# One PEER layer, 128 blocks of H: sixteen spilled blocks change operand form, and eight more blocks are spilled

## The chip, the cores and the metric

The kernel runs on one core of one Trainium2 chip. The metric is the device time of one execution in microseconds (us); the median of the runs counts, and lower is better.

## The reference, cut to what matters

Two transformer blocks on 512 tokens with d = 1024. The first ends in a PEER layer, a mixture of 16384 single-neuron experts, and the change lies there:

```python
def peer_sublayer(h, g_ffn, w_peer_q, keys_1, keys_2, peer_u, peer_v):
    x = rmsnorm(h, g_ffn)
    q = (x @ w_peer_q).reshape(T, 8, 128)                  # 8 heads
    s1, s2 = q[..., :64] @ keys_1.T, q[..., 64:] @ keys_2.T  # 128 scores each
    v1, i1 = lax.top_k(s1, 16); v2, i2 = lax.top_k(s2, 16)
    cand = v1[..., :, None] + v2[..., None, :]             # 256 candidates
    sc, ci = lax.top_k(cand, 16)
    eidx = i1[ci // 16] * 128 + i2[ci % 16]                # 128 experts per token
    gates = softmax(sc)
    act = gelu(einsum('td,tkd->tk', x, peer_u[eidx]))
    return einsum('tk,tkd->td', gates * act, peer_v[eidx])
```

## The kernel before, in words

The last 384 tokens (`ND`; the first 128 are `T0`) go through the layer densely. For each of 128 blocks `j` of 128 experts a block of H, `gelu(U_j x)`, 128 x 384, is formed, multiplied by a dense matrix of gates, and multiplied by `V_j` into the output. The first 128 tokens gather their rows of U and V one by one with indirect DMAs (`gather`, `gstep`), paced along the rest.

`hblock` forms one block of H: `wload` loads 512 KB of U and splits it into a high half (a cast, L166, on ScalarE = ACT) and a low half (a subtraction, L167, on GpSimd = POOL or on VectorE = DVE), `mm3` (L185 to L187) multiplies three pairs of halves, high x high, low x high and high x low, in 8 steps over d: 24 matmuls of 128x384 with operands of the split type, float32r. ACT applies gelu (L716). A block that is formed ahead of its turn is *spilled*: `hspill` writes it to DRAM (`h_d`), and the main loop reads it back. `SP` spreads the numbers of the spilled blocks evenly over the 128. For spilled blocks the subtraction is on POOL.

The stages around the change follow one another in `phase2`:

- **norm_apply** (L215 ff.) multiplies the residual by gain and norm for each half of the tokens: `hf`, a temporary in the ring of the H blocks (tag `hg`, 8 buffers), from which the halves `xnh` (L222, ACT) and `xnl` (L223, DVE) of the whole x are made.
- **Query stage**: 8 heads. A 512-column product with `w_pq` gives q; for each of 4 token tiles the scores (L808, native float32, 256 columns) are copied by ACT (L810) and DVE selects the 16 largest of each 128 (`top16`, L783 to L788). After heads 2 and 5 (`QH`) one block is spilled. After head 3, `xg` is built by ACT and POOL for the first 128 tokens and transposed to `xt`.
- **Index decoding**: for each of 4 token tiles DVE adds candidates (L848), selects 16 of 80 for each head, and turns their places into expert numbers by a chain of small operations (L865 to L895). At four places of each tile (`TK_H`) a block is spilled: 16 blocks. `spread` transposes indices and gates of a tile for the next stage.
- **One-hot stage**: for each of 48 groups of 8 tokens DVE builds one-hot matrices A (L920) and B (L940), 128x2048 in fp16, and TensorE multiplies them (L928) into the dense gates, which go to DRAM (`g_d`). After every second group a block is spilled: 24 blocks. A has 4 buffers, B has 3.
- 6 more blocks (`TR_H`), and then the **main loop** over the 128 j: `stage_a` forms a block or reads a spilled one, `stage_b` multiplies by gates and splits V, `stage_c` (L990) runs 18 matmuls of 512 columns.

2 + 16 + 24 + 6 = 48 blocks (`NS`) are spilled. A scheduler sets the order of each engine's instructions from this program and the pools: U's raw buffers ("row") are 3, its halves 3 (`UB`), the accumulators of H ("mm") 2.

Of the kernel before, what the change touches and what calls it, by code (L numbers as in the profile page):

```python
# [9 lines left out]
F32 = mybir.dt.float32  # L10
# [5 lines left out]
AF = mybir.ActivationFunctionType  # L16
OP = mybir.AluOpType
# [143 lines left out]
def psum(S, tag, bufs, shape=(128, 512), name=None):  # L161
    return S.ps.tile([128, 512], F32, name=name or tag, tag=tag, bufs=bufs)
# [7 lines left out]
def wload(S, pool, src, kc, m, tag="w", raw=2, bufs=2, rtag=None, eng=None):  # L170
    nc = S.nc
    r = pool.tile([128, kc * m], F32, name=tag + "r", tag=rtag or tag + "r", bufs=raw)
    nc.sync.dma_start(r, src.rearrange("p k m -> p (k m)"))
    hi = pool.tile([128, kc * m], F32R, name=tag + "h", tag=tag + "h", bufs=bufs)
    lo = pool.tile([128, kc * m], F32R, name=tag + "l", tag=tag + "l", bufs=bufs)
    split(S, hi, lo, r, eng)
    f = lambda t: t.rearrange("p (k m) -> p k m", m=m)
    return f(hi), f(lo)


def mm3(S, out, w, x, kc, xs, ws=slice(None)):

    mm = S.nc.tensor.matmul
    for k in range(kc):
        mm(out, w[0][:, k, ws], x[0][:, k, xs], start=k == 0, stop=False)  # L185
        mm(out, w[0][:, k, ws], x[1][:, k, xs], start=False, stop=False)  # L186
        mm(out, w[1][:, k, ws], x[0][:, k, xs], start=False, stop=k == kc - 1)  # L187
# [27 lines left out]
def norm_apply(S, R, hs, nr, a, sh, hi, lo, get):  # L215

    nc = S.nc
    col = lambda k: 0.0 if sh is None else sh[:, k:k + 1]
    for k in range(8):
        t = get()  # L220
        nc.vector.scalar_tensor_tensor(t, R[:, k, hs], a[:, k:k + 1], nr, op0=OP.mult, op1=OP.mult)
        nc.scalar.activation(hi[:, k, hs], t, AF.Identity, bias=col(k))  # L222
        nc.vector.scalar_tensor_tensor(lo[:, k, hs], t, col(k), hi[:, k, hs].bitcast(F32), op0=OP.add, op1=OP.subtract)  # L223
# [426 lines left out]
ND = 384  # L650
T0 = 128
GT, GJ, GPB = 32, 4, 3
HGB, NR, NG, VRB = 8, 3, 5, 5
LA, LB = 5, 4
LT = 3
QH = (2, 5)
PQE = 1
UB = 3
LATE = 7
TK_H = (2, 6, 8, 9)  # L660
TK_G = ()
TR_H = 6
G_H = 1
G_G = 0
NS = len(QH) + 4 * len(TK_H) + ND // 16 * G_H + TR_H
SP = [i * NJ // NS for i in range(NS)]


# [24 lines left out]
def phase2(S, ctx, R, gains, early=lambda S: None):  # L693

    nc, tc, ap = S.nc, S.tc, S.ap
    mm, V = nc.tensor.matmul, nc.vector
    pools = ExitStack()
    pool = lambda n, st=pools: st.enter_context(tc.tile_pool(name=n, bufs=1, reuse_waits="tile"))
    pu, xn = S.pu, S.xn
# [5 lines left out]
    nc.gpsimd.memset(yt, 0.0)  # L705
    g_d = S.dr.tile([ND // GT, 128, NJ, GT], F32, name="g_d")
    h_d = S.dr.tile([NJ, 128, ND], F32, name="h_d")
    for x, hs in enumerate(HALF):
        norm_apply(S, R, hs, S.nr[x], gains, None, xn[0], xn[1], lambda: pu.tile([128, ND], F32, name="hf", tag="hg", bufs=HGB)[:, :256])

    def hblock(j, eng=None):
        w = wload(S, pu, ap["u"][j], 8, 128, tag="u", raw=NR, bufs=UB, rtag="row", eng=eng)
        p = psum(S, "mm", 2)[:, :ND]
        mm3(S, p, w, xn, 8, slice(T0, 512))
        hg = pu.tile([128, ND], F32, name="hg", tag="hg", bufs=HGB)
        S.last_gelu = nc.scalar.activation(hg, p, AF.Gelu)  # L716
        return hg

    nh = [0]

    def hspill(n=1):
        for _ in range(n):
            nc.sync.dma_start(h_d[SP[nh[0]]], hblock(SP[nh[0]], nc.gpsimd))
            nh[0] += 1

    def gather(k, src, s):
# [34 lines left out]
    def gstep(n=1):  # L761
        for _ in range(n):
            x = next(gs, None)
            if x:
                x[0](x[1])
                gdone[0] += 1

    with tc.tile_pool(name="tk", bufs=1, reuse_waits="tile") as pt_:
# [9 lines left out]
        with tc.tile_pool(name="tq", bufs=1, reuse_waits="tile") as pq:  # L778
            T = lambda tag, n, b=2, dt=F32: pq.tile([128, n], dt, name=tag, tag=tag, bufs=b)
# [12 lines left out]
            for h in range(8):  # L792
                if h == 0:
                    ps = [psum(S, "mm", 2) for _ in range(2)]
                    for hs in HALF:
                        for w, p in zip(S.first, ps):
                            mm3(S, p[:, hs], w, xn, 8, hs)
                if h < 2:
                    p = ps[h]
                else:  # L800
                    w = wload(S, pu, ap["w_pq"][h], 8, 128, tag="u", raw=NR, bufs=UB, rtag="row", eng=PQE and nc.gpsimd)
                    p = psum(S, "mm", 2)
                    mm3(S, p, w, xn, 8, slice(None))
                qT = T("qT", 512)
                nc.scalar.copy(qT, p)
                for t in range(4):
                    p = psum(S, "st", 2)
                    mm(p[:, :256], qT[:, 128 * t:128 * t + 128], kb, start=True, stop=True)  # L808
                    s = pq.tile([128, 256], F32, name="s", tag="s", bufs=4)
                    nc.scalar.copy(s, p[:, :256])  # L810
                    for e in range(2):
                        top16(s[:, 128 * e:128 * e + 128], 128, VV[t][:, e, h], II[t][:, e, h])
                if h in QH:
                    hspill()
                if h == 3:
                    for k in range(8):
                        t = T("xg", 128, 3)
                        nc.scalar.mul(t, R[:, k, :T0], gains[:, k:k + 1])
                        nc.gpsimd.tensor_tensor(t, t, S.nr[0][:, :T0], op=OP.mult)
                        if k % 4 == 0:  # L820
                            p = psum(S, "pt", 1)
                        nc.tensor.transpose(p[:, 128 * (k % 4):128 * (k % 4) + 128], t, S.ident)
                        if k % 4 == 3:
                            nc.scalar.copy(xt[:, 128 * (k - 3):128 * (k + 1)], p)

# [17 lines left out]
            for t in range(4):  # L843
# [8 lines left out]
                for h in range(8):  # L852
                    hs = slice(16 * h, 16 * h + 16)
                    top16(cand[:, h], 80, sc[:, hs], ci[:, hs])
                    if h in TK_H:
                        hspill()
                    if late and h == LATE:
                        spread(top[0])
                    if t and h in TK_G:
                        anchor[0] = None  # L860
                        gstep()
# [20 lines left out]
                for e in range(2):  # L882
                    eq = pq.tile([128, 128, 16], BF, name="eq", tag="eq", bufs=1)
                    V.tensor_tensor(eq, abb[:, e, :, None].to_broadcast([128, 128, 16]), iob[:, None, :16].to_broadcast([128, 128, 16]), op=OP.is_equal)
                    if 8 + e in TK_H:
                        hspill()
                    if t and 8 + e in TK_G:
                        gstep()
                    e4 = eq.rearrange("p (h k) a -> p h k a", k=16)
                    V.tensor_tensor(e4, e4, IB[:, e, :, None, :].to_broadcast([128, 8, 16, 16]), op=OP.mult)  # L890
                    for n in (8, 4, 2):
                        V.tensor_tensor(eq[:, :, :n], eq[:, :, :n], eq[:, :, n:2 * n], op=OP.add)
                    V.tensor_tensor(e12[e][:, :, None], eq[:, :, 0:1], eq[:, :, 1:2], op=OP.add)
# [14 lines left out]
                else:  # L908
                    late.append((t, e12, gt))
                    if t == 3:  # L910
                        spread()

        tg = ExitStack()
        pt_ = pool("tg", tg)
        tok = lambda x, t: x[:, t // 8].rearrange("p e (r q) -> p (e r) q", q=2)[:, :, None, :].to_broadcast([128, 8, 128, 2])
# [18 lines left out]
        for n in range(ND // 8 + 1):  # L934
            if n < ND // 8:
                t, b = T0 + 8 * n, n % (GT // 8)
# [15 lines left out]
    hspill(TR_H)  # L952
    assert nh[0] == NS

    ngl = 256 - gdone[0]
    with tc.tile_pool(name="pv", bufs=1, reuse_waits="tile") as pv:
# [47 lines left out]
        get = lambda: pv.tile([128, 1024], F32, name="ys", tag="vr", bufs=VRB)  # L1004
        ys = [yt, None, None, None]
        for x, hs in enumerate(HALF):
# [6 lines left out]
            for k in range(0, 8, 2):  # L1013
                p = psum(S, "mm", 2)
# [93 lines left out]
def open3(S):  # L1108

    nc, g3 = S.nc, S.g3  # L1110
    S.p3 = ExitStack()
    pool = lambda n: S.p3.enter_context(S.tc.tile_pool(name=n, bufs=1, reuse_waits="tile", side="right"))
    S.pn = pn = pool("p3n")
    S.pw = pool("p3w")
    S.ng3 = pn.tile([128, N_GAINS3], F32, name="ng3")
    nc.vector.tensor_scalar(S.ng3, g3, -1.0, None, op0=OP.mult)
    S.modb = pn.tile([128, 48], F32, name="modb")
    nc.vector.tensor_tensor(S.modb, S.mod, g3[:, :48], op=OP.add)
    S.ga = []
    for e, g in ((1, G_N1), (4, G_N2)):  # L1120
        a = pn.tile([128, 8], F32, name=f"ga{e}")
        nc.vector.tensor_scalar(a, S.modb[:, 8 * e:8 * e + 8], 1.0, -1.0, op0=OP.add, op1=OP.mult)
        nc.vector.tensor_tensor(a, a, g3[:, g:g + 8], op=OP.mult)
        S.ga.append(a)
    S.hf = lambda: pn.tile([128, 256], F32, name="hf", tag="hf", bufs=3)
    S.hf()
    S.first = [wload(S, S.pw, S.ap["w_in2"][4 + e], 8, 128, raw=RAW) for e in range(2)]

# [320 lines left out]
```

## Time and profile before

| | |
|---|---|
| median of 3 runs | 2544.19 us (2543.97 to 2545.87) |
| profiled execution | 2549.88 us, span 2548.1 us, mean granted TensorE clock 0.984 |
| TensorE (PE) busy | 2443.6 us, 96% of the span |
| VectorE (DVE) busy | 1807.9 us, 71% |
| ScalarE (ACT) busy | 1050.5 us, 41% |
| GpSimd (POOL) busy | 651.9 us, 26% |
| DMA | 439.59 MB read, 45.09 MB written, 190 GB/s over the span |

In the span of the profiled execution the query stage lies at about 592 to 667 us, index decoding at 667 to 797, the one-hot stage at 797 to 955, and the main loop's matmuls of L990 at 998 to 1846. Busy shares over the whole span average stages in which different engines work without a pause.

### The profile page before, as it was taken

How to read it: one execution, taken by the hardware profiler on the slowest of the kernel's cores; microseconds unless marked ns; L12 is line 12 of the kernel's file. 1: busy time of each engine (PE TensorE's matmuls, PEld its weight loads, DVE VectorE, ACT ScalarE, POOL GpSimd, SP SyncE). 2: the span in 40 equal slices, each digit the busy share in tenths (PEclk: the TensorE clock that was granted, in tenths of full speed). 3: DMA queues.
4: the chain of work that ended last, by engine and by line, in shares of the span. 5: the costliest groups of instructions: out<-in, count | busy, mean ns of one | idle time of the engine just before them, and what ended most of it. 6: DMA issues, size and time to landing. Idle time of an engine off the chain costs nothing.

```text
span 2548.1 us, 35084 instructions
## 1 busy us (share of the span) xinstructions
PE 2443.6 (96%) x13173; PEld 2078.4 (82%) x13173; DVE 1807.9 (71%) x3335; ACT 1050.5 (41%) x1727; POOL 651.9 (26%) x440
## 2 busy tenths in 40 slices
PE   7999999999966799999999999999999999999999
PEld 6778888788856689888888888888877777888887
DVE  6666777659999784888887877878655655755532
ACT  5664333544333454333333333333353663544421
POOL 2101111123344563444443443444100001000000
PEclk9999999999988899999999999999999999999999
DMA  5213664651335569999999999998321212222332
GB/s 202 76 41 131 200 205 159 211 186 64 111 103 162 234 235 349 353 361 341 327 329 327 335 328 333 317 334 311 115 76 34 79 54 75 71 95 91 97 103 89
DMA packets 188538, 486.99 MB, mean 191 GB/s; under 512 B 16359, under 2 KB 81272, under 8 KB 186704
## 3 DMA queue, kind: packets, MB, share of 16 engines
q1 hardware_dynamic: 148736, 341.74, 39.8%
q0 software_dynamic: 39632, 143.00, 15.6%
q8 instruction: 103, 1.69, 0.3%
q14 instruction: 67, 0.55, 0.1%
HBM read 439.59 MB, written 45.09 MB: 190 GB/s over the span
## 4 chain that ended last, share of the span: by engine, by line
PE 82%; DVE 12%; ACT 2%; DMA 1%; POOL 1%; issue 1%; SPq 0%; DVEq 0%; ACTq 0%; POOLq 0%
PE mm L185 13%; PE mm L186 13%; PE mm L187 13%; PE sq L990 7%; PE st L990 7%; PE o L990 3%; PE pt L990 3%; PE st L186 2%; PE st L185 2%; PE st L187 2%; PE mm L1417 2%; PE mm L1416 2%; PE mm L1418 2%; PE st L928 1%; PE o L454 1%
## 5 line engine op out<-in xcount | busy, mean ns | idle before, releaser
L185 PE MATMUL mm<-xnh,uh 128*128 128x384 f32 (+2 forms) x1104 | 379.8, 344 | 17.9 <-ACT hg L716 17.9
L187 PE MATMUL mm<-xnh,ul 128*128 128x384 f32 (+2 forms) x1104 | 380.0, 344 | 11.8 <-POOL ul L167 11.8
L186 PE MATMUL mm<-xnl,uh 128*128 128x384 f32 (+2 forms) x1104 | 379.4, 344 | 0.1
L166 ACT CAST uh<-ur 128x1024 fp32r<-128x1024 f32 x136 | 143.0, 1053 | 318.5 <-PE mm L186 228.4
L167 DVE TENSOR_TENSOR wl<-wr,wh 128x1024 fp32r<-128x1024 f32 (+2 forms) x132 | 147.9, 1121 | 177.5 <-ACT wh L166 176.7
L728 POOL DMA_INDIRECT gr<-in_u_rows,iu x128 | 184.7, 1443 | 233.3 <-DVE yt L745 180.4
L728 POOL DMA_INDIRECT gr<-in_v,iv x128 | 176.9, 1382 | 233.6 <-DVE gr L741 193.7
L185 PEld LDWEIGHTS mm<-xnh,uh 128*128 128x128 f32 x1104 | 212.1, 192 | 23.6 <-ACT hg L716 18.6
L187 PEld LDWEIGHTS mm<-xnh,ul 128*128 128x128 f32 x1104 | 212.0, 192 | 14.4 <-POOL ul L167 12.4
L186 PEld LDWEIGHTS mm<-xnl,uh 128*128 128x128 f32 x1104 | 212.3, 192 | 5.9 <-DVE xnl L223 0.4
L166 ACT CAST wh<-wr 128x1024 fp32r<-128x1024 f32 (+2 forms) x132 | 126.7, 961 | 210.3 <-PE mm L1417 87.7
L167 POOL TENSOR_TENSOR ul<-ur,uh 128x1024 fp32r<-128x1024 f32 x54 | 171.2, 3180 | 140.6 <-ACT uh L166 139.5
L166 ACT CAST wh<-gj 128x384 fp32r<-128x384 f32 x128 | 65.7, 513 | 292.6 <-issue 150.2
L745 DVE SCALAR_TENSOR_TENSOR yt<-gr,act,yt 128x1024 f32<-128x1024 f32 x128 | 163.9, 1281 | 0.2
L167 DVE TENSOR_TENSOR vl<-vr,vh 128x1024 fp32r<-128x1024 f32 x128 | 156.0, 1219 | 4.4 <-ACT vh L166 4.0
L186 PE MATMUL mm<-xnl,wh 128*128 128x512 f32 (+2 forms) x400 | 156.4, 392 | 0.5 <-DVE xnl L223 0.4
L185 PE MATMUL mm<-xnh,wh 128*128 128x512 f32 (+2 forms) x400 | 156.6, 392 | 0.2 <-ACT wh L166 0.2
L741 DVE SCALAR_TENSOR_TENSOR gr<-gr,xt 128x1024 f32<-128x1024 f32 x128 | 155.7, 1219 | 0.4 <-DMA gr<-in_u_rows,iu 0.4
L187 PE MATMUL mm<-xnh,wl 128*128 128x512 f32 (+2 forms) x400 | 154.8, 388 | 0.5 <-DVE wl L167 0.5
L167 DVE TENSOR_TENSOR wl<-gj,wh 128x384 fp32r<-128x384 f32 x128 | 71.1, 556 | 115.5 <-ACT wh L166 102.3
L167 DVE TENSOR_TENSOR ul<-ur,uh 128x1024 fp32r<-128x1024 f32 x82 | 100.5, 1226 | 56.7 <-ACT uh L166 46.1
L166 ACT CAST vh<-vr 128x1024 fp32r<-128x1024 f32 x128 | 134.8, 1053 | 4.7 <-issue 3.3
(729 smaller groups left out, 6080.3 us busy)
## 6 DMA issues: line engine op xcount, KB each, us to landing
ur<-in_u SPq DMA_DIRECT2D x128, 512.0 KB
vr<-in_v SPq DMA_DIRECT2D x128, 512.0 KB
adaw<-in_w_ada SPq DMA_DIRECT2D x48, 512.0 KB
g_d<-gb SPq DMA_DIRECT2D x12, 2048.0 KB
gp<-g_d SPq DMA_DIRECT2D x32, 768.0 KB
wr<-in_w_in SPq DMA_DIRECT2D x45, 512.0 KB
wr<-in_w_up SPq DMA_DIRECT2D x44, 512.0 KB
wgr<-in_w_in SPq DMA_DIRECT2D x24, 512.0 KB
```

What stands on the lines that cost most here:

```text
L166: S.nc.scalar.copy(hi, src)
L167: (eng or S.nc.vector).tensor_tensor(lo, src, hi.bitcast(F32), op=OP.subtract)
L185: mm(out, w[0][:, k, ws], x[0][:, k, xs], start=k == 0, stop=False)
L186: mm(out, w[0][:, k, ws], x[1][:, k, xs], start=False, stop=False)
L187: mm(out, w[1][:, k, ws], x[0][:, k, xs], start=False, stop=k == kc - 1)
L728: op = nc.gpsimd.indirect_dma_start(out=r, out_offset=None, in_=src, in_offset=bass.IndirectOffsetOnAxis(ap=idx[k][:, s:s + 1], axis=0))
L741: paced(V.scalar_tensor_tensor(r, r, 1.0, xt, op0=OP.mult, op1=OP.mult, accum_out=act[:, s:s + 1]))
L745: paced(V.scalar_tensor_tensor(yt, r, act[:, s:s + 1], yt, op0=OP.mult, op1=OP.add))
L990: mm(Y[2 * t + e], W[w_][:, c], vv[v_][:, 512 * e:512 * e + 512], start=n == 0 and w_ + v_ == 0, stop=n == NJ - 1 and w_ == 1)
L1416: mm(p, w[0][:, k], gb[2 * f], start=f == 0, stop=False)
L1417: mm(p, w[0][:, k], gb[2 * f + 1], start=False, stop=False)
L1418: mm(p, w[1][:, k], gb[2 * f], start=False, stop=f == 21)
```

## The change

The blocks spilled in the query stage go from one after heads 2 and 5 to 0, 1, 1, 2, 1, 2, 1, 2 after the eight heads: 10 instead of 2, so 56 in all, and the main loop forms 72 blocks and reads 56. The 16 blocks of the decoding stage go through a new `hblock_whole`: it neither casts nor subtracts, and multiplies the raw U with the whole normalised x in 8 matmuls of native float32. That x must now be kept: `norm_apply` writes it to a tile `xr`, 128x8x512 float32, in a pool of its own that is closed before the one-hot stage's pool opens. The transposes after head 3 read `xr`, so `xg` and its sixteen operations are gone.

```diff
     for k in range(8):
-        t = get()
+        t = get(k)
         nc.vector.scalar_tensor_tensor(t, R[:, k, hs], a[:, k:k + 1], nr, op0=OP.mult, op1=OP.mult)
...
-QH = (2, 5)
+QH = (0, 1, 1, 2, 1, 2, 1, 2)
...
-NS = len(QH) + 4 * len(TK_H) + ND // 16 * G_H + TR_H
+NS = sum(QH) + 4 * len(TK_H) + ND // 16 * G_H + TR_H
...
+    xrs = ExitStack()
+    xr = xrs.enter_context(tc.tile_pool(name="xr", bufs=1, reuse_waits="tile", side="right")).tile([128, 8, 512], F32, name="xr")
     for x, hs in enumerate(HALF):
-        norm_apply(S, R, hs, S.nr[x], gains, None, xn[0], xn[1], lambda: pu.tile([128, ND], F32, name="hf", tag="hg", bufs=HGB)[:, :256])
+        norm_apply(S, R, hs, S.nr[x], gains, None, xn[0], xn[1], lambda k: xr[:, k, hs])
...
+    def hblock_whole(j):
+
+        w = pu.tile([128, 8, 128], F32, name="ur", tag="row", bufs=NR)
+        nc.sync.dma_start(w, ap["u"][j])
+        p = psum(S, "mm", 2)[:, :ND]
+        for k in range(8):
+            mm(p, w[:, k], xr[:, k, T0:], start=k == 0, stop=k == 7)
+        hg = pu.tile([128, ND], F32, name="hg", tag="hg", bufs=HGB)
+        S.last_gelu = nc.scalar.activation(hg, p, AF.Gelu)
+        return hg
...
-    def hspill(n=1):
+    def hspill(n=1, whole=False):
         for _ in range(n):
-            nc.sync.dma_start(h_d[SP[nh[0]]], hblock(SP[nh[0]], nc.gpsimd))
+            j = SP[nh[0]]
+            nc.sync.dma_start(h_d[j], hblock_whole(j) if whole else hblock(j, nc.gpsimd))
             nh[0] += 1
...
-                if h in QH:
-                    hspill()
+                hspill(QH[h])
                 if h == 3:
                     for k in range(8):
-                        t = T("xg", 128, 3)
-                        nc.scalar.mul(t, R[:, k, :T0], gains[:, k:k + 1])
-                        nc.gpsimd.tensor_tensor(t, t, S.nr[0][:, :T0], op=OP.mult)
...
-                        nc.tensor.transpose(p[:, 128 * (k % 4):128 * (k % 4) + 128], t, S.ident)
+                        nc.tensor.transpose(p[:, 128 * (k % 4):128 * (k % 4) + 128], xr[:, k, :T0], S.ident)
...
                     if h in TK_H:
-                        hspill()
+                        hspill(whole=True)
...
                     if 8 + e in TK_H:
-                        hspill()
+                        hspill(whole=True)
...
+        xrs.close()
         tg = ExitStack()
```

The order of instructions moves on two engines. On VectorE, at the end of the first phase, L197 and L198 make the norm of one half of the tokens (`nr_5064` the first half, `nr_5065` the second), L622 adds to the residual (16 of these for the second half), and L221 and L223 belong to `norm_apply`. Before:

```order
L197 SCALAR_TENSOR_TENSOR yw<-sq,yw 128x256 [waits Activation_49]
L198 SCALAR_TENSOR_TENSOR nr_5064<-yw 128x256 [waits DVE_49]
L622 TENSOR_TENSOR resid<-xres,mm 128x256 [waits PE_49]
L221 SCALAR_TENSOR_TENSOR hf<-resid,ngf,nr_5064 128x256 [waits DVE_49]
L221 SCALAR_TENSOR_TENSOR hf<-resid,ngf,nr_5064 128x256 x2
L223 SCALAR_TENSOR_TENSOR xnl<-hf,xnh 128x256 [waits Activation_49] x3
L221 SCALAR_TENSOR_TENSOR hf<-resid,ngf,nr_5064 128x256
L622 TENSOR_TENSOR resid<-xres,mm 128x256 [waits PE_49]
L221 SCALAR_TENSOR_TENSOR hf<-resid,ngf,nr_5064 128x256
L223 SCALAR_TENSOR_TENSOR xnl<-hf,xnh 128x256 [waits Activation_49]
L221 SCALAR_TENSOR_TENSOR hf<-resid,ngf,nr_5064 128x256
L223 SCALAR_TENSOR_TENSOR xnl<-hf,xnh 128x256 [waits Activation_49]
```

and after the change (the rest of the sixteen L622 stand above):

```order
L197 SCALAR_TENSOR_TENSOR yw<-sq,yw 128x256 [waits Activation_49]
L198 SCALAR_TENSOR_TENSOR nr_5064<-yw 128x256 [waits DVE_49]
L622 TENSOR_TENSOR resid<-xres,mm 128x256 [waits PE_49] x2
L786 CAST iob<-ioi 128x128 [waits Pool_49]
L790 CAST io_5517<-ioi 128x256
L197 SCALAR_TENSOR_TENSOR yw<-sq,yw 128x256 [waits Activation_49]
L198 SCALAR_TENSOR_TENSOR nr_5065<-yw 128x256 [waits DVE_49]
L221 SCALAR_TENSOR_TENSOR xr<-resid,ngf,nr_5064 128x256 [waits DVE_49,PE_49]
L221 SCALAR_TENSOR_TENSOR xr<-resid,ngf,nr_5064 128x256 x2
L223 SCALAR_TENSOR_TENSOR xnl<-xr,xnh 128x256 [waits Activation_49] x3
L221 SCALAR_TENSOR_TENSOR xr<-resid,ngf,nr_5064 128x256 x3
```

Of the sixteen L221, the eight of the first half stood among the last additions to the residual; now all stand behind the second half's norm, and the first also waits for TensorE, whose tiles held the place of `xr`.

On GpSimd, in the decoding stage, `ul` (L167) is the subtraction for one block, `IB` and `sh` (L845 and L863, after the change L855 and L873) open a token tile's decoding and its chain of small operations, and `gT` belongs to `spread`. Before:

```order
L845 CAST IB<-II_5540 128x256
L167 TENSOR_TENSOR ul<-ur,uh 128x1024 x3
L863 COPY sh<-ci 128x128
L167 TENSOR_TENSOR ul<-ur,uh 128x1024 x4
L845 CAST IB<-II_5541 128x256
L167 TENSOR_TENSOR ul<-ur,uh 128x1024
L863 COPY sh<-ci 128x128
L167 TENSOR_TENSOR ul<-ur,uh 128x1024 x4
L845 CAST IB<-II_5542 128x256
L167 TENSOR_TENSOR ul<-ur,uh 128x1024
L863 COPY sh<-ci 128x128
L841 TENSOR_TENSOR gT<-gt,gT 128x16x8
```

After:

```order
L167 TENSOR_TENSOR ul<-ur,uh 128x1024 x15
L855 CAST IB<-II_5528 128x256
L873 COPY sh<-ci 128x128
L855 CAST IB<-II_5529 128x256
L873 COPY sh<-ci 128x128
L855 CAST IB<-II_5530 128x256
L873 COPY sh<-ci 128x128
L851 TENSOR_TENSOR gT<-gt,gT 128x16x8
L855 CAST IB<-II_5531 128x256
L873 COPY sh<-ci 128x128
L851 TENSOR_TENSOR gT<-gt,gT 128x16x8
L167 TENSOR_TENSOR ul<-ur,uh 128x1024 x3
```

Between the first `IB` and the second-last `gT` no subtraction is left; the query stage's subtractions all stand ahead of it, and three of the one-hot stage's come before the last `gT`.

## Rows read from the trace of the kernel before

**Rows 1.** The chain that ended last, of the page: shares by engine

```profile
PE 82%; DVE 12%; ACT 2%; DMA 1%; POOL 1%; issue 1%; SPq 0%; DVEq 0%; ACTq 0%; POOLq 0%
```

**Rows 2.** Busy us of each engine by stretch of the span; x counts instructions

```profile
core 0: us, PE busy (x) PEld busy (x) DVE busy (x) ACT busy (x) POOL busy (x), PEclk, DMA share, GB/s
592.20:667.20 75.00, 72.96 (x346) 60.60 (x345) 74.84 (x510) 31.61 (x63) 30.44 (x19) 1.00 0.27 87
667.20:797.20 130.00, 84.48 (x433) 82.59 (x433) 128.51 (x408) 38.52 (x54) 49.54 (x28) 0.83 0.35 105
797.20:954.90 157.70, 133.47 (x1171) 122.90 (x1169) 137.37 (x97) 74.48 (x130) 90.94 (x25) 0.91 0.64 236
997.80:1845.50 847.70, 847.58 (x4160) 754.89 (x4160) 670.66 (x855) 306.52 (x422) 353.14 (x253) 1.00 0.90 319
```

**Rows 3.** VectorE's groups in 667.2 to 797.2 us: busy us, mean ns

```profile
L865 DVE TENSOR_SCALAR sh<-ci 128x128 uint32<-128x128 uint32 x16 | 12.0, 808 | 0.0
L877 DVE TENSOR_TENSOR ab<-ab,fl 128x128 f32<-128x128 f32 x8 | 8.4, 1044 | 0.0
L876 DVE TENSOR_SCALAR fl<-ab 128x128 f32<-128x128 f32 x8 | 5.8, 729 | 0.0
```

**Rows 4.** VectorE in order of time, around two sets of line 865

```profile
677.92 5.08 DVE L865 TENSOR_SCALAR sh<-ci 128x128 uint32<-128x128 uint32 x4
...
711.46 0.72 DVE L865 TENSOR_SCALAR sh<-ci 128x128 uint32<-128x128 uint32 x4
```

**Rows 5.** The splits on POOL in 667.2 to 797.2 us: min/median/max ns, first, last

```profile
L167 POOL TENSOR_TENSOR ul<-ur,uh x19: 2339/2406/4193, 666.1 to 796.8; 128x1024 fp32r<-128x1024 f32 x19
```

**Rows 6.** Two lines on VectorE, same stretch: min/median/max ns of their instructions

```profile
L877 DVE TENSOR_TENSOR ab<-ab,fl x8: 268/293/2364, 688.1 to 784.9; 128x128 f32<-128x128 f32 x8
...
L876 DVE TENSOR_SCALAR fl<-ab x8: 203/224/2265, 687.8 to 784.6; 128x128 f32<-128x128 f32 x8
```

**Rows 7.** VectorE in order of time: rows of the second half's norm

```profile
582.55 1.36 DVE L221 SCALAR_TENSOR_TENSOR hf<-resid,ngf,nr 128x256 f32<-128x256 f32 x3
...
588.03 0.99 DVE L223 SCALAR_TENSOR_TENSOR xnl<-hf,xnh 128x256 fp32r<-128x256 f32 x2
```

**Rows 8.** ScalarE in order of time: the second half's norm begins

```profile
579.70 0.47 ACT L194 ACTIVATE yw<-sq,epst 128x256 f32<-128x256 f32 x1 [0.37 <-PE sq L644]
```

**Rows 9.** TensorE in order of time: start us, us, line

```profile
591.09 1.13 PE L808 MATMUL st<-kb,qT 128*128 128x256 f32 x4
...
633.25 0.70 PE L808 MATMUL st<-kb,qT 128*128 128x256 f32 x2
...
666.50 0.33 PE L185 MATMUL mm<-xnh,uh 128*128 128x384 f32 x1
...
670.66 0.33 PE L185 MATMUL mm<-xnh,uh 128*128 128x384 f32 x1
```

**Rows 10.** Native float32 matmuls, two lines of the code: min/median/max ns of a record

```profile
L808 PE MATMUL st<-kb,qT x64: 378/379/483, 591.1 to 654.0; 128*128 128x256 f32 x64
...
L324 PE MATMUL sq<-sq,cg x6: 591/592/697, 32.6 to 42.7; 128*128 128x512 f32 x6
```

**Rows 11.** VectorE's costliest group in 797.2 to 955 us: mean ns | idle before

```profile
L920 DVE TENSOR_TENSOR A<-eT,io 128x2048 f16<-128x2048 f16 x48 | 77.4, 1614 | 20.3 <-PE st L928 20.3
```

**Rows 12.** VectorE in order of time: first and last of twenty back to back

```profile
825.55 1.21 DVE L920 TENSOR_TENSOR A<-eT,io 128x2048 f16<-128x2048 f16 x1
...
847.12 1.22 DVE L940 TENSOR_TENSOR B<-gT,A 128x2048 f16<-128x2048 f16 x1
```

**Rows 13.** POOL's splits in 796.8 to 955 us

```profile
L167 POOL TENSOR_TENSOR ul<-ur,uh 128x1024 fp32r<-128x1024 f32 x19 | 84.0, 4427 | 79.1 <-ACT uh L166 79.0
```

**Rows 14.** Busy us by stretch of ten us; PEclk is the granted clock

```profile
700.00:710.00 10.00, 0.00 (x0) 0.00 (x0) 10.00 (x46) 0.00 (x0) 3.14 (x2) 0.72 0.17 52
710.00:720.00 10.00, 6.25 (x24) 6.26 (x25) 9.97 (x38) 4.36 (x6) 5.25 (x3) 0.59 0.23 52
720.00:730.00 10.00, 10.00 (x60) 10.00 (x59) 10.00 (x17) 4.45 (x7) 7.53 (x2) 1.00 0.62 190
```

More of the change, by code (lines that the diff above doesn't have):

```diff
@@ L1124, in open3 @@
         S.ga.append(a)
-    S.hf = lambda: pn.tile([128, 256], F32, name="hf", tag="hf", bufs=3)
+    S.hf = lambda k=0: pn.tile([128, 256], F32, name="hf", tag="hf", bufs=3)
     S.hf()
```

## Prediction

> **What bounds the kernel now.** I read the chain that ended last first, and then cut the span into stages. The chain [rows 1] is TensorE for 82% and VectorE for 12%. The second number matters here: 12% of 2548.1 us is 306 us, and the stages that the change touches are about as long. The windows [rows 2] show where. In the query stage (75.0 us) VectorE is busy for 74.84 and TensorE for 72.96: both nearly full, VectorE ahead. In the decoding stage (130 us) VectorE is busy for 128.51 and TensorE for 84.48: VectorE alone sets the length. In the one-hot stage (157.7 us) neither is full. In the main loop (847.7 us) TensorE is busy for 847.58 at full clock: it is bound by TensorE, and every matmul taken out of it is time.
>
> Next, what VectorE's time in decoding is made of. One set of four shifts of line 865 takes 5.08 us, another 0.72 [rows 4]. In the first, POOL runs subtractions for spilled blocks, 2.4 us each [rows 5]. 5.08 - 0.72 is 4.36 us for two of them, 2.2 us each. Over the stage, line 865 takes 12.0 us for its 16 [rows 3]; at the free pace they would take 4 x 0.72 = 2.9. Lines 877 and 876 take 8.4 and 5.8 us for 8 each [rows 3], where their quickest, 268 and 203 ns, would make 2.1 and 1.6; their slowest, 2364 and 2265 ns, are 2.1 us longer [rows 6]. So VectorE is held while POOL subtracts, once for almost every one of the stage's 19 subtractions, of which the first and the last reach past its ends.
>
> The Trainium skill, page "SBUF — State Buffer", section "SBUF: two separate sides", says that GpSimd and VectorE share a port pair as an exclusive lock for a whole instruction. The stalled sets agree. By that rule alone a hold could last all of 2.4 us, and 18 of them 43 us.
>
> **The change, part by part.** The sum is made against the profiled execution, 2549.9 us, which is 0.22% above the median of the runs.
>
> *Start of the query stage.* The first half's L221 ran among the last additions to the residual. The order shows all sixteen now behind the second half's norm. Its eight pairs of L221 and L223 took from 582.55 to 589.02 us [rows 7], 0.81 a pair, and that norm starts on ScalarE at 579.70 [rows 8]. Now the first half's leftovers don't stand before its end, so the first L221 comes somewhat sooner, at 582, and sixteen pairs end at 595 instead of 589: 6 us. That is the high bound; where pairs run as fast as the order lets them they overlap more, and TensorE's head-0 product, which follows them step by step, makes some up. The wait for TensorE's last matmul of the phase, new in the order, ends before this norm can. What is late next is the first scores (591.09, [rows 9]) and the first selections behind them. **+5 us** (3 to 6).
>
> *Query stage.* VectorE's selections fill its 75.0 us [rows 2], 9.4 a head. With ten blocks TensorE becomes the bound. A split block is 24 matmuls from 666.50 to 670.66 [rows 9], 4.15 us. The 512-column product of a head is by columns 4.15 x 512 / 384 = 5.5, and four scores are two to four times 0.70, some of it overlapped: about 1.4 [rows 9]. With about 0.8 of waits a head with one block takes 11.8 us and with two 16.0. The order puts eight of the ten blocks ahead of the last head's scores. So these come at 2.4 + 4 x 11.8 + 2 x 16.0 = 82 us after the start, and VectorE ends about 10 later, at 92 instead of 76: **+15.5** (8 to 20). Eight subtractions more on POOL don't hold the selections: there VectorE is at its pace, full, beside POOL's 30.44 us of work [rows 2].
>
> *Decoding stage.* All 16 subtractions of its blocks and 16 casts are gone, and the order shows none left on POOL before the last `gT` but three. 18 stalls x 2.2 us would be 39. By the 2.1 us of [rows 6] 18 make 37, and I take that: **-37** (-30 to -39), *if* TensorE doesn't take VectorE's place.
>
> For that the native block must be priced, and before has no native matmul of 384 columns. Scores of 256 columns are two records of 379 ns each, and records of 512 columns take 592 ns [rows 10]: 213 ns more for 256 columns, 0.32 us for 384, two records a matmul, 0.64, eight of them 5.1 us. That is the low bound. The high bound takes the whole time of a lone pair, 0.70 us [rows 9], and 0.21 more for 128 columns in two records: 0.91, eight of them 7.3. I take 5.2, since four records in a row took 1.13 us [rows 9], so that most of a record's time is latency that the next one covers. This is dearer for TensorE than a split block, 4.15: the change buys VectorE's time with TensorE's.
>
> With 5.2, TensorE begins the natives at about 90 us after the start (last scores, then the last two split blocks), and ends 16 x 5.2 = 83 and some 6 of spread transposes later, at 179. VectorE ends at 92 + 130 - 37 = 185. A margin of 6 us: it is gone when a native costs 5.6.
>
> *One-hot stage.* Twenty operations in a row start 21.57 us apart, first to last [rows 12], 1.135 each: 96 would take 109 us. The stage took 157.7 [rows 2], with 20.3 us idle for L928 [rows 11]. That leaves 28 us of holds (line 920 averages 1614 ns [rows 11], not 1135), as long as 13 of the 19 subtractions on POOL [rows 13]. Before, a part of the 24 subtractions had run by the stage's start, or was left past its end. After, TensorE is free of backlog, the order alternates blocks and products evenly, and all but a few run here. 109 + 26 x 2.15 = 165: **+7.5** (-7 to +15). This is the softest term. POOL's own subtractions average 4427 ns here against a median of 2406 in decoding [rows 13, 5]: each side waits for the other, so the hold per subtraction may be less than 2.15.
>
> *Main loop.* Blocks past the last product and before the loop's first L990 stay 9 in the order. Eight blocks fewer at 4.15 us, in a stage where TensorE is never idle: **-33** (-28 to -35). Eight reloads of 196 KB replace 512 KB of U, so the DMA moves less, but in a shorter time: share 0.90 [rows 2] becomes about 0.94. `xg`'s sixteen operations were beside VectorE's selections and cost nothing then or now.
>
> Sum: 5 + 15.5 - 37 + 7.5 - 33 = -42. 2549.9 - 42 = 2508, and less 0.22%, **2502 us** for the median. Adding the ranges of the terms with some compensation between stages, 2490 to 2515.
>
> **Rivals.** 0.2% of this kernel, 5.1 us, is about what a measurement of it can tell from no change.
>
> *Slower: native matmuls at the lower clock.* After VectorE-bound idling TensorE is granted less than full clock: in 700 to 710 us PE does nothing and the clock is 0.72, in the next ten 0.59, and only in the third, with PE full, 1.00 [rows 14]. If the natives ran throughout at 1.2 GHz, one would cost 2 x 5.1 = 10.2 us, TensorE's part of decoding would end at 90 + 163 + 6 = 259, 74 us past VectorE, and the sum would be +32: about 2576. From 5.6 us per native on TensorE sets the stage's end, each 0.1 us more costs 1.6 us, and at 5.6 + 42 / 16 = 8.2 the gain is gone; the high bound of 7.3 gives 2529. Against it: with 83 us of natives in 93 us TensorE has little left to idle, and the query stage before it runs at 1.00 [rows 2]. The Trainium skill, page "TensorE: Matmul & The Clock Gate", section "Part 1: The HAM clock gate", says the engine starts throttled and is released by activity; the three windows agree. Chance 0.09.
>
> *No change: the holds aren't POOL's doing or don't leave.* If the slow operations were slow by themselves (banks, DMA traffic), decoding would keep its 130 us, with TensorE's natives well under VectorE: 5 + 15.5 + 7.5 - 33 = -5, about 2539. Against it stands the set of 0.72 us [rows 4], in a window where POOL has no subtraction. Chance 0.09.
>
> *Faster still: one-hot without holds.* If the even order lets A and B run at their own pace or TensorE set it (a block of 4.15 us and two products of 16 matmuls, 128 columns each, by columns 1.85: 24 times 6.0 is 144, and some waits), and the stage ends at 151 to 154 instead of 165, the sum is -54 to -56: 2488. For it speaks that POOL was the one to wait in places [rows 13]; against it the 28 us of holds that before paid. Chance 0.14.
>
> *Half a main loop.* If the reads at DMA share 0.94 come late and each reloaded block gives back some 1.5 us, the loop gains only 20: 2515. It had 0.90 without a gap on TensorE [rows 2]. Chance 0.15.
>
> **How the numbers follow.** The forecast has 0.50; the four rivals 0.09, 0.09, 0.14 and 0.15; 0.03 is left for what I didn't see. The range 2478 to 2536 takes in the forecast, the last two rivals and the natives up to 7.7 us: about 0.82. Faster by over 0.2%: 0.50 + 0.14 + 0.15 + a part of the other two (natives under 7.9, holds partly gone) = 0.85; within 0.2%: 0.06; slower: 0.09.
>
> **What would show it.** In the changed kernel: no subtraction on POOL during decoding, the set of line 865 (now another number) at 0.72 us in all four tiles, decoding some 93 us long with VectorE full; native blocks of about 5.2 us from first to first; the query stage some 92 us with TensorE full and VectorE idle; one-hot about 165; the first L990 near 988; the loop near 815 and still full. I am wrong if natives exceed 5.6 us, if VectorE waits in decoding for scores that come late, or if the loop shows TensorE waiting for reloaded blocks.

## The result, and the profile after

The changed kernel takes 2509.33 us (median of 4 runs, 2505.52 to 2510.91) against 2544.38 in the same job: ratio 0.9859, 95% interval 0.9842 to 0.9876. Run again in another job, as a zero for experiments, it gave 2507.77 and 0.9841 (0.9828 to 0.9854). Faster by 1.4 to 1.6%; 2502 was forecast.

The profiled execution took 2509.95 us, 39.9 less than that of before. The page's busy line and its chain (PEld is the loading of TensorE's weights):

```profile
span 2507.8 us, 34802 instructions
PE 2451.0 (98%) x13045; PEld 2050.2 (82%) x13045; DVE 1788.6 (71%) x3327; ACT 1032.6 (41%) x1703; POOL 622.1 (25%) x424
PE 84%; DVE 12%; ACT 2%; DMA 1%; issue 1%; POOL 0%; SPq 0%; DVEq 0%; ACTq 0%; POOLq 0%
```

The windows of the changed kernel, by the same four stages as [rows 2] (query, decoding, one-hot, main loop):

```profile
core 0: us, PE busy (x) PEld busy (x) DVE busy (x) ACT busy (x) POOL busy (x), PEclk, DMA share, GB/s
600.00:690.10 90.10, 89.76 (x443) 78.32 (x443) 75.74 (x510) 33.61 (x62) 33.95 (x16) 1.00 0.33 108
690.10:788.60 98.50, 85.51 (x263) 49.97 (x261) 97.37 (x408) 23.90 (x38) 12.11 (x12) 0.95 0.40 121
788.60:946.20 157.60, 151.94 (x1312) 137.96 (x1313) 157.09 (x97) 81.71 (x142) 86.95 (x29) 0.99 0.73 267
987.70:1805.40 817.70, 817.58 (x3985) 724.46 (x3984) 663.83 (x855) 296.40 (x411) 364.51 (x253) 1.00 0.92 328
```

Read the pair PE and DVE in each row. In the query stage they have changed places: TensorE is full, VectorE has 14 us to spare. In decoding VectorE is still full, but needs 97.37 us instead of 128.51 for the same 408 instructions. In the one-hot stage VectorE is now full without a gap. The main loop is full on TensorE as before.

Stage boundaries go by instructions: first selection, first candidates, first A, last B, first and last matmul of the main loop's product line. By these:

| | before | after | change | forecast |
|---|---|---|---|---|
| first selection at | 592.3 | 600.0 | +7.7 | +5 |
| query stage | 74.6 | 90.1 | +15.5 | +15.5 |
| decoding | 130.3 | 98.5 | -31.8 | -37 |
| one-hot | 157.8 | 157.6 | -0.2 | +7.5 |
| to the first product of the loop | 42.8 | 41.5 | -1.3 | 0 |
| main loop | 851.5 | 817.7 | -33.8 | -33 |
| after it | 698.8 | 702.4 | +3.6 | 0 |
| span | 2548.1 | 2507.8 | -40.3 | -42 |

The last stage holds nothing of the change; over all kernels traced here it lies between 696.6 and 702.4, so its +3.6 is scatter. The first selection scatters too, from 598.1 to 601.4 in the runs whose start is that of the changed kernel.

VectorE's groups in decoding that answer to [rows 3] (busy us, mean ns; the line numbers are 10 higher):

```profile
L875 DVE TENSOR_SCALAR sh<-ci 128x128 uint32<-128x128 uint32 x16 | 2.9, 240 | 0.0
L887 DVE TENSOR_TENSOR ab<-ab,fl 128x128 f32<-128x128 f32 x8 | 2.4, 298 | 0.1
L886 DVE TENSOR_SCALAR fl<-ab 128x128 f32<-128x128 f32 x8 | 1.7, 215 | 0.0
```

12.0 us has become 2.9, 8.4 has become 2.4, 5.8 has become 1.7: the free pace that was read from their quickest instructions [rows 4, 6]. POOL's subtractions from the first candidates to the last B (min/median/max ns, first, last start):

```profile
L167 POOL TENSOR_TENSOR ul<-ur,uh x26: 2347/3425/3452, 776.2 to 943.9; 128x1024 fp32r<-128x1024 f32 x26
```

The first starts at 776.2 us, 86 us into decoding. Three of the one-hot stage's blocks come ahead of its start at 788.6 and hold VectorE there. One line of VectorE in decoding (start us, us), beside no subtraction and then beside these:

```profile
733.23 0.38 DVE L903 TENSOR_TENSOR e<-eq 128x128 f32<-128x128 bf16 x1
...
776.59 2.35 DVE L903 TENSOR_TENSOR e<-eq 128x128 f32<-128x128 bf16 x1
...
786.34 2.35 DVE L903 TENSOR_TENSOR e<-eq 128x128 f32<-128x128 bf16 x1
```

TensorE in decoding (start us, us, line; two records make a matmul, 16 a block):

```profile
689.66 51.76 PE L727 MATMUL mm<-xr,ur 128*128 128x384 f32 x160
...
746.55 23.10 PE L727 MATMUL mm<-xr,ur 128*128 128x384 f32 x64 [4.80 <-ACT hg L729]
...
769.81 10.49 PE L727 MATMUL mm<-xr,ur 128*128 128x384 f32 x32
```

Ten native blocks in 51.76 us are 5.18 us each, at full clock; 5.2 was taken. TensorE ends its natives at 780 and VectorE the stage at 788.6, a margin of 8.

### The profile page after: what moved, and what is told of

Read it like the earlier page. It is cut to its first block, busy times and chain, and to the rows that moved or that the text cites. A ratio compares the mean times of both kernels' runs of the same rounds, so it can differ in the third digit from the quotient of the medians.

```text
span 2507.8 us, 34802 instructions
## 1 busy us (share of the span) xinstructions
PE 2451.0 (98%) x13045; PEld 2050.2 (82%) x13045; DVE 1788.6 (71%) x3327; ACT 1032.6 (41%) x1703; POOL 622.1 (25%) x424
## 4 chain that ended last, share of the span: by engine, by line
PE 84%; DVE 12%; ACT 2%; DMA 1%; issue 1%; POOL 0%; SPq 0%; DVEq 0%; ACTq 0%; POOLq 0%
PE mm L185 14%; PE mm L186 14%; PE mm L187 14%; PE sq L1001 7%; PE st L1001 7%; PE o L1001 3%; PE pt L1001 3%; DVE A L931 3%; PE st L186 2%; PE st L185 2%; PE st L187 2%; DVE B L951 2%; PE mm L1429 2%; PE mm L1428 2%; PE mm L1427 2%; PE o L454 1%
## 5 line engine op out<-in xcount | busy, mean ns | idle before, releaser
L185 PE MATMUL mm<-xnh,uh 128*128 128x384 f32 (+2 forms) x976 | 332.6, 342 | 0.0
L187 PE MATMUL mm<-xnh,ul 128*128 128x384 f32 (+2 forms) x976 | 331.7, 340 | 0.0
L186 PE MATMUL mm<-xnl,uh 128*128 128x384 f32 (+2 forms) x976 | 330.6, 339 | 0.0
L167 DVE TENSOR_TENSOR wl<-wr,wh 128x1024 fp32r<-128x1024 f32 (+2 forms) x132 | 147.8, 1120 | 178.4 <-ACT wh L166 177.7
L166 ACT CAST uh<-ur 128x1024 fp32r<-128x1024 f32 x120 | 126.3, 1053 | 317.9 <-PE mm L186 186.1
L742 POOL DMA_INDIRECT gr<-in_u_rows,iu x128 | 190.6, 1489 | 204.3 <-DVE yt L759 150.6
L186 PEld LDWEIGHTS mm<-xnl,uh 128*128 128x128 f32 x976 | 184.7, 189 | 5.3
L185 PEld LDWEIGHTS mm<-xnh,uh 128*128 128x128 f32 x976 | 184.4, 189 | 4.9
L187 PEld LDWEIGHTS mm<-xnh,ul 128*128 128x128 f32 x976 | 184.2, 189 | 2.1
L167 POOL TENSOR_TENSOR ul<-ur,uh 128x1024 fp32r<-128x1024 f32 x46 | 132.7, 2887 | 153.0 <-ACT uh L166 129.6
L167 DVE TENSOR_TENSOR vl<-vr,vh 128x1024 fp32r<-128x1024 f32 x128 | 156.0, 1219 | 3.4 <-ACT vh L166 3.2
L167 DVE TENSOR_TENSOR wl<-gj,wh 128x384 fp32r<-128x384 f32 x128 | 71.1, 555 | 111.8 <-ACT wh L166 102.3
L167 DVE TENSOR_TENSOR ul<-ur,uh 128x1024 fp32r<-128x1024 f32 x74 | 90.6, 1225 | 38.6 <-ACT uh L166 33.9
```

Of the source, the lines that this page charges most:

```text
L166: S.nc.scalar.copy(hi, src)
L167: (eng or S.nc.vector).tensor_tensor(lo, src, hi.bitcast(F32), op=OP.subtract)
L742: op = nc.gpsimd.indirect_dma_start(out=r, out_offset=None, in_=src, in_offset=bass.IndirectOffsetOnAxis(ap=idx[k][:, s:s + 1], axis=0))
```

## The experiments

All compare a kernel with the kernel before, in the same job; times of stages are from their traces. The first four were run together.

**Native form alone.** The query stage spills two blocks again.

```diff
-QH = (0, 1, 1, 2, 1, 2, 1, 2)
+QH = (0, 0, 1, 0, 0, 1, 0, 0)
```

> Native blocks in decoding stay, the query stage spills 2 blocks again instead of 10 (48 in all). Theory H (POOL's subtractions hold VectorE; natives free it; each block formed in the query stage costs there 1.95 us and saves 4.15 in the main loop): the query stage goes back from 90.6 to about 75 us, decoding stays near 98, the main loop is 33 us longer than in the changed kernel: about 2509 - 15.6 + 33 = 2527 us, 17 faster than before. Rival S (the eight more spilled blocks paid, the native form did not): decoding gains nothing and the later start costs 7: about 2551.

2525.43 us, ratio 0.9901 (0.9883 to 0.9919). Query stage and decoding:

```profile
598.10:672.40 74.30, 70.75 (x296) 53.44 (x295) 74.27 (x509) 22.98 (x48) 14.87 (x8) 1.00 0.25 75
672.40:771.40 99.00, 78.14 (x246) 47.78 (x245) 97.68 (x408) 22.65 (x36) 15.08 (x12) 0.91 0.40 119
```

The query stage is 15.8 us shorter than in the changed kernel, decoding is the same, the main loop takes 851.5, as before the change. Rival S would have left decoding at 130.

**More spilled blocks alone.** Decoding's blocks are split on POOL again.

```diff
-                        hspill(whole=True)
+                        hspill()
```

(at both places)

> Ten blocks in the query stage, but decoding's 16 blocks split on POOL again (56 in all; x is still kept whole for the transposes). Theory H: VectorE is held again, decoding goes from 98 back to 127 to 131 us, the rest as in the changed kernel: about 2509 + 32 = 2541. Rival S: decoding as in the changed kernel, about 2509.

2540.93 us, 0.9967 (0.9953 to 0.998). Decoding takes 130.5 us, the main loop 819.1. So of the 33 us that the eight blocks gain in the main loop some 16 go into the query stage and 7 into its later start (x is still kept), and 8 are left without the native form; each part is worth what the theory gave it.

**A subtraction on POOL that nobody needs.** The native blocks stay.

```diff
+        lo = pu.tile([128, 1024], F32R, name="ul", tag="ul", bufs=UB)
+        r = w.rearrange("p k m -> p (k m)")
+        nc.gpsimd.tensor_tensor(lo, r, r, op=OP.subtract)
         p = psum(S, "mm", 2)[:, :ND]
```

> The changed kernel with native blocks, and beside each of decoding's 16 native blocks one subtraction of 128x1024 float32 on POOL (raw U less itself) whose result nobody reads. Nothing else changes: no cast on ACT, no matmul. Theory H: each holds VectorE for about 2.1 us, decoding is 32 to 35 us longer: 2541 to 2544. Rival C (casts on ACT, the split matmuls or the transfers slowed VectorE's operations, not POOL): decoding keeps its 98 us, 2509 to 2512.

2529.80 us, 0.9924 (0.991 to 0.9939): decoding 120.0 us, 21.5 more, neither the 32 to 35 of H nor C's zero. The trace shows why it is less. POOL's added subtractions in decoding (min/median/max ns, first, last):

```profile
L727 POOL TENSOR_TENSOR ul<-ur x13: 1887/1915/3141, 699.5 to 785.4; 128x1024 fp32r<-128x1024 f32 x13
```

They are 13, three having run during the selections, and with one tensor read twice they take 1.9 us instead of 2.4. 13 x (1.9 - 0.25 of the held operation's own) is 21.5. One of them, on POOL and then on VectorE (start us, us):

```profile
734.55 1.95 POOL L727 TENSOR_TENSOR ul<-ur 128x1024 fp32r<-128x1024 f32 x1 [1.89 <-DMA ur<-in_u]
```

```profile
734.55 0.21 DVE L889 TENSOR_SCALAR fl<-ab 128x128 f32<-128x128 f32 x1
734.68 0.08 DVE L801 MATCH_VALUE_LOAD ci<-sc,cand 128x8 f32 x1
734.75 0.23 DVE L801 FIND_INDEX8 ci<-sc,cand 128x8 uint32<-128x80 f32 x1
734.90 1.76 DVE L890 TENSOR_TENSOR ab<-ab,fl 128x128 f32<-128x128 f32 x1
736.58 0.08 DVE L803 MATCH_VALUE_LOAD s<-sc,cand 128x8 f32 x1
```

The search instructions go on while POOL works, each at its usual length; line 889, which starts together with POOL, keeps its length too. The first two-operand instruction waits until POOL's end at 736.50 and takes 1.76 us instead of 0.3. This is the hold, with no cast, split matmul or other transfer added.

**Split blocks with VectorE's own subtraction.**

```diff
-    def hspill(n=1, whole=False):
+    def hspill(n=1, whole=False, eng=nc.gpsimd):
...
-            nc.sync.dma_start(h_d[j], hblock_whole(j) if whole else hblock(j, nc.gpsimd))
+            nc.sync.dma_start(h_d[j], hblock_whole(j) if whole else hblock(j, eng))
...
-                        hspill(whole=True)
+                        hspill(eng=None)
```

> Decoding's 16 blocks are split, with the subtraction on VectorE itself instead of POOL (the query and one-hot stages' stay on POOL). Theory H: no holds, but VectorE does the 16 subtractions at about 1.2 us each: decoding 98 + 19 = 117 us, about 2528. TensorE has 4.15 instead of 5.3 us a block and is not the bound. Rival C: the split form itself slows VectorE's small operations, so decoding is at 130 + 19, about 2560.

2524.46 us, 0.9904 (0.9887 to 0.9922): decoding 115.4 us. That is 16.9 more than with native blocks, for 15 subtractions of 1.2 us in the stage, as H has it; the split form itself does no harm. Half of what the native form wins in decoding could have been had by moving the subtraction from POOL to VectorE.

The next three shared a job with the second run of the changed kernel:

> The changed kernel itself once more, as the zero of the other runs of this chip. All theories: as before, ratio to the kernel before 0.984 to 0.988. If the ratio is nearer to 0.984, the 5.5 us between the profiled execution of the kernel before and its median was chance, and the gain is the 40 us of the traces; if it stays at 0.986, the median's 35 us stands.

0.9841: see above. The medians of the kernel before in the four jobs were 2544.4, 2549.3, 2547.0 and 2549.2 us, so its profiled 2549.9 was within their scatter.

**The first half's norm back in its place.**

```diff
-def norm_apply(S, R, hs, nr, a, sh, hi, lo, get):
+def norm_apply(S, R, hs, nr, a, sh, hi, lo, get, keep=None):
...
+        if keep:
+            nc.scalar.copy(keep(k), t)
...
-        norm_apply(S, R, hs, S.nr[x], gains, None, xn[0], xn[1], lambda k: xr[:, k, hs])
+        norm_apply(S, R, hs, S.nr[x], gains, None, xn[0], xn[1], lambda k: xr[:, k, hs] if x else pu.tile([128, ND], F32, name="hf", tag="hg", bufs=HGB)[:, :256], None if x else lambda k: xr[:, k, hs])
```

> The first half of the tokens is normalised into the temporary hf again, as before the change, and ACT copies it to xr; the second half goes to xr directly. Theory H: the first half's eight L221 run again among the last additions to the residual, the first selection comes at 593 to 595 us instead of 600, about 6 us are won: ratio about 0.0023 below the changed kernel's. Rival P (the later start is made by the transposes from xr and the throttled clock at 580 to 590 us, or the copies on ACT cost as much): no gain, within 2 us.

2501.08 us, 0.982 (0.9807 to 0.9834): 6.7 us faster than the changed kernel in that job. VectorE in order of time in the changed kernel, around the norm:

```profile
583.04 1.28 DVE L221 SCALAR_TENSOR_TENSOR xr<-resid,ngf,nr 128x256 f32<-128x256 f32 x3
...
595.67 0.43 DVE L223 SCALAR_TENSOR_TENSOR xnl<-xr,xnh 128x256 fp32r<-128x256 f32 x1 [0.49 <-ACT xnh L222]
600.03 0.49 DVE L797 MAX8 VV<-s 128x8 f32<-128x128 f32 x2 [3.94 <-ACT s L824]
```

and with the first half in `hf`:

```profile
575.42 1.27 DVE L221 SCALAR_TENSOR_TENSOR hf<-resid,ngf,nr 128x256 f32<-128x256 f32 x3
...
586.37 2.77 DVE L223 SCALAR_TENSOR_TENSOR xnl<-xr,xnh 128x256 fp32r<-128x256 f32 x8
593.90 0.49 DVE L799 MAX8 VV<-s 128x8 f32<-128x128 f32 x2 [4.76 <-ACT s L826]
```

The first selection comes 6 us sooner: the later start is the order of VectorE's sixteen pairs, as the order had shown.

**The one-hot stage's subtractions on VectorE.** `hspill` as in the split experiment, and

```diff
-                hspill(G_H)
+                hspill(G_H, eng=None)
```

> In the one-hot stage the 24 blocks' subtractions go to VectorE instead of POOL. Theory H: a subtraction on POOL costs VectorE 2.2 us there, one of its own 1.2, so VectorE needs 5.75 us for two pairs of A and B and a block instead of 6.75; TensorE needs about 6.4 and becomes the bound: the stage gets 5 to 8 us shorter, ratio about 0.0025 below the changed kernel's. Rival D (the holds overlap with waits, and a subtraction in VectorE's queue waits for ACT's cast and stalls A and B behind it): no gain, or up to 10 us slower.

2496.28 us, 0.9807 (0.9794 to 0.982), 11.5 us faster than the changed kernel: more than the 5 to 8 that were expected. The one-hot stage:

```profile
786.80:933.10 146.30, 142.71 (x1268) 133.76 (x1267) 136.82 (x118) 78.67 (x135) 13.42 (x7) 1.00 0.74 272
```

VectorE falls from 157.09 to 136.82 us and TensorE, busy for 142.71 of 146.30, becomes the bound. TensorE needs about 6.0 us for two products and a block, not the 6.4 of the expectation, which held waits. What the holds look like in the changed kernel, POOL and then VectorE:

```profile
815.90 3.44 POOL L167 TENSOR_TENSOR ul<-ur,uh 128x1024 fp32r<-128x1024 f32 x1 [3.29 <-ACT uh L166]
```

```profile
815.88 1.21 DVE L951 TENSOR_TENSOR B<-gT,A 128x2048 f16<-128x2048 f16 x1
817.02 3.40 DVE L931 TENSOR_TENSOR A<-eT,io 128x2048 f16<-128x2048 f16 x1
820.35 1.21 DVE L951 TENSOR_TENSOR B<-gT,A 128x2048 f16<-128x2048 f16 x1
```

POOL's 3.44 us are about 1.1 of waiting for B and 2.35 of its own; then A waits for POOL, 3.40 instead of 1.21. Each waits for the whole instruction of the other, and VectorE loses 2.2 us a block.

**Three more native blocks.**

```diff
-NS = sum(QH) + 4 * len(TK_H) + ND // 16 * G_H + TR_H
+NS = sum(QH) + 4 * len(TK_H) + 3 + ND // 16 * G_H + TR_H
...
-                    if h in TK_H:
+                    if h in TK_H or t and h == 4:
```

> Three more native blocks in decoding, one in each of the last three token tiles: 59 spilled. In the changed kernel TensorE idles 13 us in decoding (4.8 and 8.3). Theory H: three natives need 16 us, so the stage grows by 3 to 8 us, and the main loop loses three blocks, 12.4 us: 5 to 9 us faster than the changed kernel. Rival M (natives are gated by the two accumulators and gelu, the idle time can't be used, or the main loop has run into the DMA): within 3 us of it.

2504.43 us, 0.9832 (0.9818 to 0.9845): 3.3 us below the changed kernel, within the scatter of both, between the two expectations. By the traces the loop is 11.6 us shorter than in the changed kernel's second run, and decoding with the one-hot stage 8.4 longer: TensorE's idle time went only in part to the natives, since a gap of 5 us on gelu stays. Decoding by itself:

```profile
690.00:782.20 92.20, 87.07 (x264) 50.83 (x263) 91.07 (x408) 20.33 (x32) 4.44 (x8) 0.96 0.41 120
```

It is 6.3 us shorter than in the changed kernel, for the same 408 instructions on VectorE: POOL's first subtraction starts here at 791.4 us, behind the stage's end, so the three holds of decoding's tail have moved into the next stage.

The last three shared a job.

**The query stage native, too.**

```diff
-                hspill(QH[h])
+                hspill(QH[h], True)
```

> The query stage's ten blocks are native, too; nothing is split on POOL there. Theory H: there TensorE is the bound, and a native block costs it 5.3 us where a split one costs 4.15: the stage grows by 10 x 1.17 = 12 us, ratio about 0.0045 above the changed kernel's. Rival F (the query stage waits for casts and subtractions, and without them TensorE gains more than the dearer matmuls cost): same or up to 5 us faster.

2512.11 us, 0.9852 (0.9837 to 0.9867), which alone doesn't tell it from the changed kernel. The trace: the query stage takes 96.6 us instead of 90.1, and the first product of the loop comes at 993.6 instead of 987.7. The sign is H's, the size half: only the blocks ahead of the last selection lengthen the stage, at most eight as the order has it (8 x 1.03 is 8), and the first native matmul starts at 598.9 us, ahead of the first selection at 599.2. What hides the last 2 us was not traced.

**Both gains, and all three.** The first half's norm with VectorE's subtractions, and the same with three more natives:

> The changed kernel with the first half's norm back in its place and the one-hot stage's subtractions on VectorE. Theory H: the two gains lie in different stages, 6.7 and 11.5 us, and add up: ratio about 0.9786, 2491 us or less. Rival: the one-hot stage's gain was TensorE's idle time that the earlier start uses as well, and only 11 to 13 us are won together.

> Both, and the three more native blocks in decoding. Theory H: with the one-hot stage bound by TensorE, three natives that end after VectorE's decoding push it back in full: 16 us less the 5 to 8 that are idle in decoding, against 12 less in the main loop; within 4 us of the kernel without them.

2492.29 us, 0.9778 (0.9765 to 0.9792), and 2490.04, 0.977 (0.9756 to 0.9783). The two gains add up: in the trace the first product of the loop comes at 971.5, 16 us sooner than in the changed kernel. The three natives on top make no difference that these runs can tell. By their ratios both kernels beat the changed one's second run by 0.6 to 0.7%.

## Why the prediction was right, and where its sizes were off

*The holds.* Right, and shown, not only argued: native blocks without a subtraction free VectorE, an idle subtraction on POOL brings the hold back, split blocks without POOL don't. The term was -37 and measured -31.8. The mis-sized step is the count: it took all 18 holds as gone (18 x 2.1 is 37.8, put down as 37) and nothing for the three subtractions that the order showed ahead of the last `gT`. These run in decoding's tail and hold VectorE for some 6 us. The kernel with three more natives, where they run later, shows it: its decoding takes 92.2 us, 38.1 less than before the change.

*The one-hot stage.* +7.5 forecast, -0.2 measured. The step "26 x 2.15" counted those three here: 26 subtractions start between the first candidates and the last B, but only 23 of them in the stage. (157.6 - 109) / 23 is 2.1 us, so the hold itself was right. The two errors, in decoding and here, are largely one: three subtractions put into the wrong stage. The rival of a one-hot stage without holds (by its own ends of 151 to 154 us a sum of -53 to -56, not -54) fell, though 157.6 lies nearer to it than to 165: the 23 holds came in full, and only with the subtractions on VectorE did the stage reach TensorE's pace, 146.3.

*Start of the query stage.* +7.7 against +5, outside the term's 3 to 6; the experiment with `hf` gives back 6. The step that failed is the discount on the 6 us that were called the high bound: nothing was made up by overlap, as the sixteen pairs went from 583.04 to 596.10 us, 0.82 each. The other 1.7 us are within the scatter of the first selection.

*Query stage and native price.* +15.5 and 5.18 us a block, both as forecast, and by the mechanism that was given: the scores of heads 2, 3 and 4 (counted from 0) start on TensorE at 614.04, 625.73 and 641.58 us, so a head with one block takes 11.7 us and one with two 15.9, against 11.8 and 16.0. The rival of the lower clock had its mechanism, not its weight: among the natives the clock fell to 0.71 in the ten us around a gap of 4.8 us (740 to 750 us), the four blocks behind the gap took 5.8 us each, and TensorE still ended ahead of VectorE.

*Main loop.* -33.8 against -33, at a DMA share of 0.92 with TensorE full. The rival of late reads fell.

*The median.* By the traces the sum was off by 2 us of 42. Its terms were not as good: without their signs their errors add up to 21 us. Decoding and one-hot stage cancel but for 2.5 us, for the reason given; that the other errors, 4.2 us the other way, come out so near to it is luck. The predicted median was 7 us too low mostly because the step "less 0.22%" carried over the distance of one profiled execution from its median. That distance was scatter: the changed kernel's profiled 2509.95 lay at its own median.

## What to carry to other kernels

When a small operation on VectorE takes two very different times, look at what POOL does at that moment: dividing the group's busy time by its quickest instruction prices the holds, and the count of POOL's instructions in the stage checks it. Then count from the order in which stage each remaining one runs. A dearer matmul was a good buy here in decoding, where TensorE had idle time beside a bound VectorE, and a loss in the query stage, where it had none. The same subtraction on VectorE itself is the cheaper remedy to try: it won 11.5 us in the one-hot stage, and in decoding half of what the native form won.

## What the runs showed that was not expected

The search instructions (MAX8, FIND_INDEX8) run at 0.23 us beside a subtraction on POOL, while two-operand instructions (1.76 us instead of 0.3), shifts (four in 5.08 us instead of 0.72) and casts (2.17 us instead of 0.48) wait for its end. A subtraction that reads one tensor twice took 1.9 us on POOL, with two tensors 2.4. And TensorE's idle time of 13 us in decoding could be filled only in part by three native blocks: they cost the two stages 8.4 us.
